# A transformer block in float32: a hand-written engine order for the first norm and for the turn to the up projection

## The chip, the cores and the metric

The kernel runs on one core of a Trainium2 chip. The metric is the device time of one launch in microseconds (us), and of several runs the median. The engines are named as the profile names them: PE is TensorE (PEld its weight loads), DVE is VectorE, ACT is ScalarE, POOL is GpSimd, SP is SyncE, which here only issues DMAs.

## The reference, cut to what matters

One block works on x of 1024 tokens by 1024 channels, all in float32: a norm, one wide projection into a gated convolution, an attention with three dilations and two gates, their merge, a second norm, and a feed-forward part with a short causal convolution.

```python
h = rms_norm(x, norm1_g)                       # first norm
z = h @ w_in
glu_in, q, k, v, gate_logits = split(z)
a = causal_depthwise_conv(a_val * sigmoid(a_gate), conv_w, conv_b)
y_a = silu(rms_norm(a, conv_norm_g)) @ w_conv_out
y_b = dilated_attention(q, k, v) @ w_attn_out
x = x + (g_a * y_a + g_b * y_b) @ w_out
h = rms_norm(x, norm2_g)                       # second norm
u = causal_depthwise_conv(h @ w_up, ffn_conv_w, ffn_conv_b)
x = x + (silu(u_gate) * u_val) @ w_down
```

## The kernel before, in words

**Products.** Each float32 operand is split into a high part (ACT copies it into the type float32r, L76) and a low part (DVE subtracts the high part, L77). A product is three matmuls: high by high, high by low, low by high (gemm_half, L103 to L111; product, L546 to L552). A weight piece of 128 by 1024 is loaded by SP into one of four buffers of the tag "raw" (stage, L79), then split.

**First norm (L197 to L224).** ACT issues a DMA that reads the norm's weights once for each of 128 partitions (gb1, L200). SP loads the eight x tiles of 128 tokens and, after the fourth, the first two weight pieces (g0, v0). For each tile ACT squares with a running sum (L221), DVE forms the mean (L100), POOL takes the power -1/2 (L101), DVE scales by it and by gb1 (L223), PE transposes eight blocks into two PSUM banks (L190), and ACT and DVE split them into the high and low halves of hT.

**Gated convolution input (L227 to L238).** For each of eight channel groups two products, glug and gluv, each in two halves of 512 tokens: half 0 needs the norm's tiles 0 to 3, half 1 tiles 4 to 7. The first channel group uses g0 and v0.

**Output projection and second norm (L522 to L543).** In the second pass over the eight token tiles, each tile's product wo goes through: DVE adds x (L533), ACT squares (L535), DVE and POOL form the factor (L538, L100, L101), DVE scales (L540). Two tiles later PE transposes the scaled tile (L515) and ACT copies it into "raws" (L516). The halves 0 and 1 of raws hold tokens 0 to 511 and 512 to 1023; with the two halves of the channels these are the four blocks b11, b21 (first tokens) and b12, b22 (last tokens).

**Up projection (L546 to L659).** It is computed in the manner of Strassen and Winograd: seven products for a two by two block of products. Its left operands are the sums t1 = b12 - b11, t3 = b22 - b12, t2 = t3 + b11 and t4 = b21 - t2, and b11, b21, b22 themselves (L594 to L621). POOL makes t1 and t4, DVE the others; each is made in two column halves (cols) and split. For each of the 22 channel tiles f, up_first loads the weight uv and makes the two products X and Z; up_sums loads ug and makes with DVE the sums s12 and two differences (s3, and a12, which becomes s4); up_rest makes the other five products, of which two are accumulated onto Y and the others onto X, and the short convolution. The sums s12 sit in a "raw" buffer too.

**Order.** Every engine runs its own queue in order. In what order the instructions are put there is decided by a scheduler when the kernel is built, from the order of the code and from its own estimates.

Of the kernel before, what the change touches and what calls it, by code (L numbers as in the profile page):

```python
# [12 lines left out]
F32 = mybir.dt.float32  # L13
# [37 lines left out]
def block_kernel(ctx: ExitStack, tc: tile.TileContext, x, g1, g2, pack, mask,  # L51
# [38 lines left out]
    def wpiece(src, name):  # L90
        raw = stage(src, name)
        hi, lo = wsplit(raw, name)
# [20 lines left out]
    def gemm_ch(ps, w, actT):  # L113
        for half in range(2):
            for _ in gemm_half(ps[:, half * 512 : half * 512 + 512], w, actT, half):
                pass
# [66 lines left out]
    def transpose_split(dst, src, tt):  # L183

        half, c0 = tt // 4, (tt % 4) * P
        for kk in range(2):
            ps = bank_ps(f"tp_{tt}_{kk}")
            for j in range(4):
                k = kk * 4 + j
                pe.transpose(ps[:, j * P : (j + 1) * P], src[:, k * P : (k + 1) * P], ident)  # L190
            psv = ps.rearrange("p (a b) -> p a b", a=4)
            hi = dst[0][half][:, kk * 4 : kk * 4 + 4, c0 : c0 + P]
            lo = dst[1][half][:, kk * 4 : kk * 4 + 4, c0 : c0 + P]
            split(hi, lo, psv)


    with tc.tile_pool(name="ph1", bufs=1) as p1:  # L197
        t4 = lambda name, dt=F32: p1.tile([P, 1024], dt, tag="t4", bufs=4, name=name)
        gb1 = p1.tile([P, D], F32, tag="csq", bufs=1, name="gb1")
        act.dma_start(gb1, bass.AP(tensor=g1.tensor, offset=g1.offset, ap=[[0, P], [1, D]]))  # L200
        xt = []
        for tt in range(8):
# [3 lines left out]
            if tt == 3:  # L206
                wfirst = [wpiece(w_ch[8], "g0"), wpiece(w_ch[0], "v0")]
        sp.dma_start(pk, pack)
        make_identity(nc, ident)
        pool.memset(mhalf, -0.5)  # L210
        pool.memset(ones, 1.0)
        dve.tensor_tensor(out=qkg, in0=pk[:, C_QG : C_QG + 1], in1=pk[:, C_KG : C_KG + 1], op=ALU.mult)
        dve.tensor_scalar(qkg, qkg, DH ** -0.5, None, op0=ALU.mult)

        hT = hb_tiles(hb1, "hT")
        for tt in range(8):
            xx = xt[tt]
            xs = t4(f"xs_{tt}")
            ss = p1.tile([P, 1], F32, tag="ss", bufs=2, name=f"ss_{tt}")
            rs = p1.tile([P, 1], F32, tag="rs", bufs=2, name=f"rs_{tt}")  # L220
            act.activation(xs, xx, AF.Square, accum_out=ss)  # L221
            rstd_of(rs, ss, D, ss)
            dve.scalar_tensor_tensor(out=xs, in0=xx, scalar=rs, in1=gb1, op0=ALU.mult, op1=ALU.mult)  # L223
            transpose_split(hT, xs, tt)  # L224
# [3 lines left out]
        for c in range(8):  # L228
            a = p1.tile([P, CW - 1 + T], F32, tag="apad", bufs=10, name=f"apad_{c}")
            pool.memset(a[:, : CW - 1], 0.0)  # L230
            gp = big_ps(f"glug_{c}")
            gemm_ch(gp, wfirst[0] if c == 0 else wpiece(w_ch[8 + c], f"g{c}"), hT)
            sg = t4(f"sg_{c}")
            act.activation(sg, gp, AF.Sigmoid)
            vp = big_ps(f"gluv_{c}")
            gemm_ch(vp, wfirst[1] if c == 0 else wpiece(w_ch[c], f"v{c}"), hT)
# [3 lines left out]
        sqacc = p1.tile([P, T], F32, name="sqacc")  # L240
# [233 lines left out]
    with tc.tile_pool(name="ph3", bufs=1) as p3:  # L474
# [46 lines left out]

        tails = []  # L522
        for j in range(2):
            wpieces = [wpiece(w_o[j, :, 2 * i : 2 * i + 2, :], f"wo{j}_{i}") for i in range(4)]
            for tt in range(8):
# [7 lines left out]
                dve.tensor_tensor(out=x2[:, cs], in0=ps, in1=x2[:, cs], op=ALU.add)  # L533
                sp.dma_start(dx2[tt][:, cs], x2[:, cs])
                act.activation(ps, x2[:, cs], AF.Square, accum_out=ss2[:, tt, j : j + 1])  # L535
                if j == 1:
                    s1 = p3.tile([P, 2], F32, tag="s1", bufs=2, name=f"s1_{tt}")
                    dve.tensor_tensor(out=s1[:, 0:1], in0=ss2[:, tt, 0:1], in1=ss2[:, tt, 1:2], op=ALU.add)  # L538
                    rstd_of(s1[:, 1:2], s1[:, 0:1], D, s1[:, 0:1])
                    dve.scalar_tensor_tensor(out=x2, in0=x2, scalar=s1[:, 1:2], in1=gb2, op0=ALU.mult, op1=ALU.mult)  # L540
# [16 lines left out]
        def up_first(f):  # L557

            v = stage(w_up[f], f"uv{f}")
            vh, vl = wsplit(v, f"uv{f}")  # L560
            xz = big_ps(f"xz_{f}")
            product(xz[:, 0:512], four(vh)[:, 0:4], four(vl)[:, 0:4], *left[0], True)
            product(xz[:, 512:1024], four(vh)[:, 4:8], four(vl)[:, 4:8], *left[1], True)
            return v, xz

        def up_sums(f, v):
            g = stage(w_up[FT + f], f"ug{f}")
            s = wp.tile([P, 1024], F32, tag="raw", bufs=4, name=f"s12_{f}")
            a11, a12, a21, a22 = v[:, 0:512], v[:, 512:], g[:, 0:512], g[:, 512:]
            s1, s2 = s[:, 0:512], s[:, 512:]  # L570
            dve.tensor_tensor(out=s1, in0=a21, in1=a22, op=ALU.add)
            dve.tensor_tensor(out=s2, in0=s1, in1=a11, op=ALU.subtract)
            sw = wsplit(s, f"s12_{f}")
            dve.tensor_tensor(out=a21, in0=a11, in1=a21, op=ALU.subtract)
            gw = wsplit(g, f"s3g_{f}")
            dve.tensor_tensor(out=a12, in0=a12, in1=s2, op=ALU.subtract)
# [12 lines left out]
        t2 = []  # L589

        def keep(n, src, q):
# [267 lines left out]
```

## Time and profile before

| | |
|---|---|
| median of 3 runs | 1815.13 us (1812.67 to 1815.44) |
| profiled execution | 1811.43 us, span 1809.6 us |
| granted TensorE clock | 0.991 |
| PE busy | 1765.8 us |
| DVE busy | 1318.8 us |
| ACT busy | 771.6 us |
| POOL busy | 195.8 us |

The span runs from the first to the last instruction. In rows of the timeline the first number is the start in us, the second the length; an "x4" at the end says that four instructions are merged, and the bracket gives the idle time before and what ended it. Rows of stretches give for each engine its busy time and, in brackets, its instructions, then the granted clock, the busy share of the DMA engines and GB/s. Rows of waits give the total, the number and the longest.

### The profile page before, as it was taken

The page shows a single profiled execution, that of the slowest core. Times are in us where ns is not written, and L with a number is a line of the kernel's source. Part 1 is how long each engine was busy: PE and PEld are TensorE (multiplying, and loading weights), DVE is VectorE, ACT ScalarE, POOL GpSimd, SP SyncE. Part 2 cuts the span into 40 slices and gives each one's busy share as a digit, 9 for nine tenths or more (in the row PEclk, how much of TensorE's full clock was granted, in tenths as well). Part 3 has the DMA queues.
Part 4 walks back from the last instruction along what each step waited for, and adds up shares of the span by engine and source line. Part 5 has one row for each costly group of instructions (what it writes and reads, how often), then busy time and mean ns, then how long its engine had stood idle before and what let it go on. Part 6 is the DMA issues. An engine that isn't in the chain of part 4 may idle for free.

```text
span 1809.6 us, 22474 instructions
## 1 busy us (share of the span) xinstructions
PE 1765.8 (98%) x8244; PEld 1461.9 (81%) x8244; DVE 1318.8 (73%) x1798; ACT 771.6 (43%) x1202; POOL 195.8 (11%) x197
## 2 busy tenths in 40 slices
PE   7999999999999999999999999989999999999999
PEld 5888888888887888887888878768888888878887
DVE  5999999999735655666654543787777777789863
ACT  4111132232245656666655332545444554543441
POOL 1000133133002122222210000210000000000000
PEclk9999999999999999999999999999999999999999
DMA  5111145345549456666527543313222222389851
GB/s 203 59 47 47 41 134 163 116 134 157 157 173 246 145 158 175 180 165 179 164 70 279 169 160 133 104 48 107 80 82 81 71 95 91 116 303 335 298 180 47
DMA packets 142063, 257.57 MB, mean 142 GB/s; under 512 B 11265, under 2 KB 60545, under 8 KB 141953
## 3 DMA queue, kind: packets, MB, share of 16 engines
q1 hardware_dynamic: 141808, 255.61, 43.8%
q8 instruction: 65, 1.06, 0.3%
q10 hardware_dynamic: 144, 0.52, 0.1%
q14 instruction: 46, 0.37, 0.1%
HBM read 190.03 MB, written 66.06 MB: 142 GB/s over the span
## 4 chain that ended last, share of the span: by engine, by line
PE 53%; DMA 4%; DVE 4%; issue 1%; ACT 1%; SPq 1%; POOLq 0%; POOL 0%; DVEq 0%; ACTq 0%
PE xz L550 5%; PE xz L551 5%; PE xz L552 5%; PE dx L703 5%; PE dy L703 5%; DMA gg<-dya 2%; PE pp L400 2%; PE y L550 2%; PE y L552 2%; PE y L551 2%; PE ya L108 2%; PE ya L109 2%; PE ya L110 2%; PE o L408 2%; PE wo L126 1%; PE wo L127 1%
## 5 line engine op out<-in xcount | busy, mean ns | idle before, releaser
L253 DVE SCALAR_TENSOR_TENSOR cacc<-apad,pk,cacc 128x1024 f32<-128x1024 f32 x240 | 297.7, 1274 | 0.7
L125 PE MATMUL qkv<-hi_qkv,hT 128*128 128x512 f32 x384 | 151.8, 396 | 0.0
L127 PE MATMUL qkv<-hi_qkv,hT 128*128 128x512 f32 x384 | 150.0, 391 | 0.0
L126 PE MATMUL qkv<-lo_qkv,hT 128*128 128x512 f32 x384 | 149.4, 390 | 0.0
L389 DVE CUSTOM_DVE_ANT_0 p<-s,m 128x128 f32<-128x128 f32 (+7 forms) x128 | 95.1, 750 | 62.7 <-PE pp L400 39.0
L77 DVE TENSOR_TENSOR pl<-pp,ph 128x512 fp32r<-128x512 f32 x192 | 103.1, 549 | 49.1 <-ACT ph L76 48.6
L393 POOL TENSOR_SCALAR p<-p,st 128x128 f32<-128x128 f32 (+7 forms) x128 | 94.9, 748 | 335.5 <-DVE st L392 211.9
L76 ACT ACTIVATE ph<-pp 128x512 fp32r<-128x512 f32 x192 | 91.3, 487 | 92.2 <-PE pp L400 89.3
L649 DVE SCALAR_TENSOR_TENSOR u<-u,pk 128x1023 f32<-128x1023 f32 (+1 forms) x88 | 112.3, 1279 | 18.9 <-ACT u L647 18.5
L101 POOL TENSOR_TENSOR rs<-ss,mhalf 128x8 f32<-128x8 f32 (+1 forms) x40 | 80.3, 2010 | 353.1 <-DVE ss L100 353.0
L391 ACT ACTIVATE p<-p,st 128x128 f32<-128x128 f32 (+7 forms) x128 | 99.0, 776 | 14.6 <-DVE st L389 12.9
L108 PE MATMUL gate<-hT,hi_gt 128*128 128x512 f32 x256 | 101.8, 398 | 0.0
L109 PE MATMUL gate<-hT,hi_gt 128*128 128x512 f32 x256 | 100.8, 394 | 0.0
L110 PE MATMUL gate<-hT,lo_gt 128*128 128x512 f32 x256 | 100.3, 393 | 0.0
L400 PE MATMUL pp<-ident,p 128*128 128x128 f32 x576 | 94.4, 277 | 0.0
L127 PEld LDWEIGHTS qkv<-hi_qkv,hT 128*128 128x128 f32 x384 | 72.0, 188 | 15.3
L126 PEld LDWEIGHTS qkv<-lo_qkv,hT 128*128 128x128 f32 x384 | 72.2, 188 | 14.5 <-DVE lo_qkv L77 0.3
L125 PEld LDWEIGHTS qkv<-hi_qkv,hT 128*128 128x128 f32 x384 | 72.2, 188 | 14.0
L400 PEld LDWEIGHTS pp<-ident,p 128*128 128x128 f32 x576 | 69.5, 142 | 10.0 <-issue 0.2
L384 PE MATMUL s<-kh,q 128*128 128x512 f32 (+1 forms) x192 | 69.7, 368 | 7.3 <-DVE st L389 4.8
L408 PE MATMUL o<-ph,v 128*128 128x512 f32 x192 | 73.1, 381 | 3.6 <-ACT ph L76 1.8
L409 PE MATMUL o<-pl,v 128*128 128x512 f32 x192 | 70.5, 369 | 1.6 <-DVE pl L77 1.5
(269 smaller groups left out, 4610.4 us busy)
## 6 DMA issues: line engine op xcount, KB each, us to landing
wr<-w_down SPq DMA_DIRECT2D x45, 512.0 KB, 5.7
gr<-dff SPq DMA_DIRECT2D x62, 256.0 KB, 5.2
raw_qkv<-w_qkv SPq DMA_DIRECT2D x24, 512.0 KB, 3.9
raw_uv<-w_up SPq DMA_DIRECT2D x22, 512.0 KB, 3.3
raw_ug<-w_up SPq DMA_DIRECT2D x22, 512.0 KB, 3.3
dff<-u SPq DMA_DIRECT2D x22, 512.0 KB, 2.6
dv<-v SPq DMA_DIRECT2D x16, 512.0 KB, 3.2
raw_gt<-w_ch SPq DMA_DIRECT2D x16, 512.0 KB, 4.8
```

The lines of the kernel that those rows point to most:

```text
L108: pe.matmul(o, hi[:, k, :], ah[:, k, :], start=(k == 0), stop=False)
L109: pe.matmul(o, hi[:, k, :], al[:, k, :], start=False, stop=False)
L110: pe.matmul(o, lo[:, k, :], ah[:, k, :], start=False, stop=(k == KT - 1))
L125: pe.matmul(ps, ah, hi[:, k % 2, :], start=(k == 0), stop=False)
L126: pe.matmul(ps, ah, lo[:, k % 2, :], start=False, stop=False)
L127: pe.matmul(ps, al, hi[:, k % 2, :], start=False, stop=(k == KT - 1))
L253: dve.scalar_tensor_tensor(out=acc, in0=a[:, j : j + T], scalar=w(j), in1=acc, op0=ALU.mult, op1=ALU.add)
L400: pe.transpose(pp[:, qb * P : (qb + 1) * P], pts[qb][:, kt * P : (kt + 1) * P], ident)
L550: pe.matmul(o, wh[:, k, :], bh[:, k, :], start=(start and k == 0), stop=False, skip_group_check=not start)
L551: pe.matmul(o, wh[:, k, :], bl[:, k, :], start=False, stop=False, skip_group_check=not start)
L552: pe.matmul(o, wl[:, k, :], bh[:, k, :], start=False, stop=(k == 3), skip_group_check=not start)
L703: pe.matmul(banks[n], a[:, c], b[:, d], start=(start and i == 0 and m == 0), stop=(stop and i == nf - 1 and m == 2), skip_group_check=True)
```

## The change

1. The first norm's weights come as one row on one partition. Two matmuls with a row of ones spread it over the partitions into PSUM, and DVE copies it into gb1 in two pieces.
2. A block with a manual schedule fixes the order on ACT, DVE and PE from there to the last tile's split: statistic, scaling and transposes of tiles 0 to 3, the splits of their first four channel blocks, the products of glug and gluv over these blocks, the other four blocks, and tiles 4 to 7 one by one. The transposes of tile 2 go to PSUM that the first products use later. The weight split of the second channel group is issued after it.
3. At the turn the last tile's addition, the last three transposes, the sums and the first three up products stand in a second manual block. The weights uv0 and uv1 are staged ahead of it. PE's transposes of tile 6 stand before the first up product. The third product (f = 2) goes to two single banks.
4. POOL makes none of the sums any more: DVE makes t1, t2 = b22 - t1, t3 and t4. The low part of b22 is made by ACT (minus the high part) and by two DMAs from the POOL queue that add b22 to it.
5. In up_sums the difference a12 is formed before s3; for f = 0 the work is cut in two.

The diff, cut to its core:

```diff
-        gb1 = p1.tile([P, D], F32, tag="csq", bufs=1, name="gb1")
-        act.dma_start(gb1, bass.AP(tensor=g1.tensor, offset=g1.offset, ap=[[0, P], [1, D]]))
+        g1r = p1.tile([1, D], F32, tag="csq", bufs=1, name="g1r")
+        act.dma_start(g1r, g1.unsqueeze(0))
...
+        with tc.manual_schedule(engines={ENG.Activation, ENG.DVE, ENG.PE}):
+            for kk in range(2):
+                ps = bank_ps(f"gb_{kk}")
+                pe.matmul(ps, ones[0:1, :], g1r[:, kk * 512 : kk * 512 + 512], start=True, stop=True)
+                dve.tensor_copy(gb1[:, kk * 512 : kk * 512 + 512], ps)
+            for tt in range(3):
+                measure(tt)
+                scaled(tt)
+                turned(tt, 0)
+                turned(tt, 1)
+            measure(3)
+            high(0, 0)
+            low(0, 0)
+            scaled(3)
+            high(0, 1)
+            low(0, 1)
+            turned(3, 0)
+            turned(3, 1)
+            for tt in (1, 2):
+                high(tt, 0)
+                low(tt, 0)
...
+            act.activation(hl[0][0], wraw[0], AF.Copy)
+            high(3, 0)
+            low(3, 0)
+            wlow(0)
+            act.activation(hl[1][0], wraw[1], AF.Copy)
+            wlow(1)
+            a, b = range(4), range(4, 8)
+            first_pair(0, a, ((0, 0),), 0)
...
+            for tt in (1, 2, 3):
+                high(tt, 1)
+                low(tt, 1)
+            measure(4)
+            scaled(4)
+            first_pair(0, b, ((0, 0),), 0)
+            first_pair(0, b, ((0, 0), (0, 1)), 1)
+            first_pair(0, b, ((0, 1), (1, 0)), 0)
+            turned(4, 0)
+            turned(4, 1)
+            first_pair(0, b, ((1, 0),), 1)
+            measure(5)
+            scaled(5)
+            for kk in range(2):
+                high(4, kk)
+                low(4, kk)
+            for tt in (5, 6):
+                turned(tt, 0)
+                turned(tt, 1)
+                measure(tt + 1)
+                scaled(tt + 1)
+                for kk in range(2):
+                    high(tt, kk)
+                    low(tt, kk)
+            turned(7, 0)
+            turned(7, 1)
+            for kk in range(2):
+                ends = high(7, kk), low(7, kk)
...
-        v0, xz0 = up_first(0)
-        transpose_raw(*tails.pop(0))
-        ready = [(v0, xz0) + up_sums(0, v0)]
...
+        pre = [stage(w_up[f], f"uv{f}") for f in range(2)]
+        pre = [(v, wsplit(v, f"uv{f}")) for f, v in enumerate(pre)]
+        with tc.manual_schedule(engines={ENG.Activation, ENG.DVE, ENG.PE}):
+            transpose_raw(*tails.pop(0))
+            add_rest(1, 7, x2, ps)
+            transpose_raw(*tails.pop(0))
+            sums(cols[0])
+            s7 = spread(7)
+            high2("t2", t2[0], cols[0])
+            low2("t2", t2[0], cols[0])
+            scale2(x2, s7)
+            v0, xz0 = up_first(0, pre[0])
+            transpose_raw(x2, 7)
+            early2 = up_sums(0, v0, 0)
+            ups = [up_first(1, pre[1]), up_first(2, None, True)]
+            sums(cols[1])
+            high2("t2", t2[1], cols[1])
+            low2("t2", t2[1], cols[1])
+            for q, t in zip(cols, t13):
+                last = high2("t1", t, q), low2("t1", t, q)
+            ready = [(v0, xz0) + up_sums(0, v0, early2)]
...
+            for q in cols:
+                high2("b22", b22[:, :, q], q)
+                lo = blocks["b22"][1][:, :, q]
+                act.activation(lo, blocks["b22"][0][:, :, q].bitcast(F32), AF.Copy, scale=-1.0)
+                pool.dma_start(lo.bitcast(F32), b22[:, :, q], accum_op=ALU.add)
```

In it measure(t) is the square on ACT, the mean on DVE and the power on POOL; scaled(t) is DVE's scaling; turned(t, k) four transposes of a tile; high and low are the two parts of a split; first_pair makes products of the first channel group over the given channel blocks; less, high2 and low2 are a subtraction on DVE and the two parts of a split of the sums.

More of the change, by code (lines that the diff above doesn't have):

```diff
@@ L111, in gemm_half, with gemm_ch @@
             yield
-    def gemm_ch(ps, w, actT):
-        for half in range(2):
+    def gemm_ch(ps, w, actT, halves=(0, 1)):
+        for half in halves:
             for _ in gemm_half(ps[:, half * 512 : half * 512 + 512], w, actT, half):
@@ L599, in sums @@
[L599 to L608 removed]
+            t = t13[q.start // 256]
+            t2.append(view(p4r.tile([P, 1024], F32, tag="st", bufs=2, name=f"cb_t2_{q.start}")))
```

200 lines of the change are left out of this document (121 added, 79 removed).

## The prediction, made before the changed kernel ran

> **What bounds the kernel now.** I read the busy table first, then stretches of the first norm and of the turn to the up projection, then the waits.
>
> ```profile
> span 1809.6 us, 22474 instructions
> PE 1765.8 (98%) x8244; PEld 1461.9 (81%) x8244; DVE 1318.8 (73%) x1798; ACT 771.6 (43%) x1202; POOL 195.8 (11%) x197
> ```
>
> TensorE (PE) is busy for 98% of the span, so the change can gain only where PE waits or runs at half clock. In the stretches the columns are length, then busy time of PE, weight loads, VectorE (DVE), ScalarE (ACT), POOL, then the granted clock.
>
> ```profile
> 9.41:20.18 10.77, 6.95 (x33) 5.58 (x33) 9.51 (x15) 9.61 (x18) 2.12 (x8) 0.85 1.03 419
> 20.18:48.21 28.03, 27.77 (x128) 22.27 (x128) 15.19 (x24) 12.07 (x19) 3.32 (x6) 0.94 0.20 70
> 1202.19:1247.19 45.00, 44.89 (x195) 36.18 (x194) 35.99 (x40) 24.52 (x28) 0.00 (x0) 1.00 0.20 71
> 1158.88:1209.90 51.02, 41.78 (x182) 32.91 (x180) 46.22 (x44) 27.75 (x36) 13.39 (x6) 0.93 0.19 65
> ```
>
> PE's first product begins at 20.18; from there to 48.21, where the second channel's product begins, PE hardly waits. The turn (1158.88 to 1209.90, the first product of up tile 2) holds 46.22 us of DVE work in 51.02: DVE bounds it. After it PE is full again. So time won or lost by 48.21 and by 1209.90 goes straight to the end; both points are the same work in both kernels.
>
> PE's pace, and the links of the norm's chain:
>
> ```profile
> 5.99 1.06 ACT L221 ACTIVATE xs<-x 128x1024 f32<-128x1024 f32 x1 [3.55 <-DMA x<-x]
> 7.17 0.15 DVE L100 TENSOR_SCALAR ss<-ss 128x1 f32<-128x1 f32 x1 [7.17 <-ACT xs L221]
> 8.07 1.28 DVE L223 SCALAR_TENSOR_TENSOR xs<-x,rs,gb 128x1024 f32<-128x1024 f32 x1 [0.75 <-POOL rs L101]
> 17.76 1.94 PE L190 MATMUL tp<-ident,xs 128*128 128x128 f32 x8 [1.94 <-DVE xs L223]
> 20.18 0.80 PE L108 MATMUL glug<-hT,hi_g 128*128 128x512 f32 x1 [0.48 <-ACT hT L76]
> 23.19 0.63 PE L110 MATMUL glug<-hT,lo_g 128*128 128x512 f32 x1
> 23.62 0.49 PE L108 MATMUL glug<-hT,hi_g 128*128 128x512 f32 x1
> 25.10 0.39 PE L108 MATMUL glug<-hT,hi_g 128*128 128x512 f32 x1
> 25.33 0.39 PE L109 MATMUL gluv<-hT,hi_v 128*128 128x512 f32 x1
> 27.60 1.91 PE L190 MATMUL tp<-ident,xs 128*128 128x128 f32 x16
> 28.24 2.06 ACT L76 ACTIVATE hT<-tp 128x512 fp32r<-128x512 f32 x4 [3.42 <-PE tp L190]
> 28.41 1.28 DVE L223 SCALAR_TENSOR_TENSOR xs<-x,rs,gb 128x1024 f32<-128x1024 f32 x1
> 29.61 2.48 DVE L77 TENSOR_TENSOR hT<-tp,hT 128x512 fp32r<-128x512 f32 x4
> 48.21 0.50 PE L108 MATMUL glug<-hT,hi_g 128*128 128x512 f32 x1
> ```
>
> A product costs 0.43 us at half clock (23.19 to 23.62) and 0.227 at full. Eight transposes cost 1.94 and some 0.8 (mean 0.1 each from the 16 in 1.91, the last's tail off). A squared tile reaches DVE 1.18 after its start (5.99 to 7.17); from there to the scaling 0.90, the scaling 1.28. A high part takes ACT 0.52 (four in 2.06), a low part DVE 0.62 (2.48 for four).
>
> **Part 1, the first norm.** *Spread weight.* The 512 KB broadcast goes, one row of 4 KB, two matmuls with ones and two DVE copies come.
>
> ```profile
> gb<-g ACTq DMA_DIRECT2D x1, 512.0 KB, 5.5
> 506.43 0.61 PE L333 MATMUL psr<-dg,ones 128*128 128x128 f32 x4
> 507.94 0.69 DVE L335 COPY sqacc<-psr 128x512 f32<-128x512 f32 x1
> ```
>
> At the stretch's 419 GB/s, 512 KB are 1.25 us: x may land 0 to 1.25 earlier; I take 1.0, so 4.9. The nearest matmuls with ones are two records each; four of 128 columns take 0.61, about 0.45 each at 512 columns, 0.9 a matmul and 1.8 at half clock. The copies (0.69) stand at the head of DVE's queue: with the row landed near 3 the second ends at about 7.3, and DVE's first statistic waits for it instead of 6.1 (4.9+1.18). Bounds 6.1 to 7.4; I take 7.3.
>
> *To the first product.* In the new order each tile is statistic, scaling, next tile: 0.90+1.28, about 2.15 with overlaps. The fourth ends at 7.3 + 3x2.15 + 2.18 = 15.9; four transposes at half clock, 0.25 of pipe and a high part (0.6) bring the first product to 17.6, not 20.18: **2.6 us won** (bounds 1.2 to 4).
>
> *After it.* The new PE order has 44 products, then tile 4's transposes, 4 products, tiles 5, 6, 7, then 48 products. 44x0.227 = 10.0, and 1.4 for the products still at half clock (seven by 0.2), end at 29.0; tile 4's first four transposes at 29.4. Now the queues bite: DVE has tile 6's scaling *behind* tile 4's low parts, and tile 7's behind tile 5's. From 29.4: pipe 0.24, two highs (1.05), the square of tile 6 queued behind them on ACT (1.18), statistic to scaling 0.90, scaling 1.3: tile 6 can be transposed at 34.05. PE has 4 products and 12 transposes till 31.45: it **waits 2.6**. Then two lows (1.25), 0.9 and 1.28: tile 7 at 37.45; PE, done at 34.85, **waits 2.6** again. High and low part of tile 7 let the half-1 products run from 39.15 and, for all but two, 40.05. Before, the last of the eight scalings was done at 29.7 (28.41+1.28), ahead of PE's need, so nothing of this was seen. 46 products take 10.4, with 0.4 for half clock: the second channel begins at 50.9. **Part 1: +2.7** (bounds +0.5 to +4).
>
> The half clock in it:
>
> ```profile
> 13.58:16.99 3.41, 1.07 (x8) 0.86 (x8) 3.41 (x5) 3.41 (x8) 0.66 (x2) 1.00 1.02 415
> 16.99:20.40 3.41, 2.17 (x9) 1.80 (x10) 3.41 (x6) 3.41 (x8) 0.38 (x2) 0.50 1.04 422
> 20.40:23.81 3.41, 3.41 (x8) 2.29 (x9) 3.41 (x7) 3.29 (x7) 0.97 (x3) 0.50 0.59 230
> ```
>
> A window with 1.07 us of PE in 3.41 is followed by half clock until one is full. PE's 0.8 between 31.45 and 34.85 is as little, so tile 7 and the first products run at half clock: 1.0 us of the +2.7. [...]
>
> **Part 2, the turn.** Before, 24 transposes (2.4) and 156 products (35.4) make 37.8 of 51.02 us, so 13.2 are lost.
>
> ```profile
> PE y L551 <- DVE blk_t L77: 4.7, 1, 4.7
> PE y L550 <- ACT hi_s L76: 2.7, 1, 2.7
> 1160.19 2.43 POOL L599 TENSOR_TENSOR cb_t<-h2raw,h2raw 128x1024 f32<-128x1024 f32 x1 [0.55 <-ACT h2raw L516]
> 1160.29 3.41 DVE L540 SCALAR_TENSOR_TENSOR x<-x,s,gb 128x1024 f32<-128x1024 f32 x1
> 1167.18 1.28 DVE L540 SCALAR_TENSOR_TENSOR x<-x,s,gb 128x1024 f32<-128x1024 f32 x1
> 1170.65 2.90 DVE L77 TENSOR_TENSOR lo_s<-raw_uv,hi_s 128x512 fp32r<-128x512 f32 x1
> 1183.83 2.80 DVE L602 TENSOR_TENSOR cb_t<-cb_t,h2raw 128x1024 f32<-128x1024 f32 x1
> 1191.80 2.75 DVE L571 TENSOR_TENSOR s<-raw_ug 128x512 f32<-128x512 f32 x1
> 1165.91 1.04 ACT L76 ACTIVATE hi_uv<-raw_uv 128x1024 fp32r<-128x1024 f32 x1
> 1166.86 1.04 ACT L76 ACTIVATE blk_t<-cb_t 128x1024 fp32r<-128x1024 f32 x1
> 1151.81 3.49 DVE L77 TENSOR_TENSOR h2left<-h2raw,h2left 128x1024 fp32r<-128x1024 f32 x3
> raw_uv<-w_up SPq DMA_DIRECT2D x1, 512.0 KB, 3.4
> ```
>
> *DVE's work.* Beside a POOL subtraction the scaling took 3.41, else 1.28. With POOL's four gone DVE gets them (4x1.14, from 3.49 for three) and loses b22's two low parts (2x1.14, now ACT and an accumulating DMA): 2.3 more. Against it stand the four stretched rows: 3.41 for 1.28, 2.90 and 2.75 where 512 columns take 0.62, 2.80 for 1.14, some 8 us less. That alone shortens the stage by several us. But the new order adds a wait.
>
> *The order, step by step.* Tiles 5 and 6 are transposed together: PE waits 0.55 for tile 6's scaling and its first up product ends at 1166.5; tile 7's scaling is ready at 1166.9, the second product ends at 1173.15. Meanwhile DVE makes the sums of tile 0's weight (1166.8 to 1168.1), ACT splits them behind tile 7's copies (1168.6), DVE makes the low part (1169.7) and a12 (ends 1171.5). **Only now may SP load the third weight, uv2**: in the program it takes the buffer of those sums, which a12 reads last, and SP waits for exactly that instruction. 3.4 us (row above; 0.1 of signal) land it at 1174.95. ACT's next instruction is uv2's high part and DVE's its low part, both queues in order: DVE stands for 4.6 us, ACT from 1169.7, PE for **2.9** (1173.15 to 1176.05) and 0.85 more for the low part. Queued behind on DVE are the second column's subtractions; behind on ACT its high part and eleven more.
>
> *Then.* DVE: low part and two subtractions, 1176.1 to 1179.7. ACT from 1179.75: seven of 1024 columns to 1186.3 (t2, t1 twice, b22 twice, its negative twice, each 0.94), s3g, s4, t4 twice, the copy of X, t3 (0.94, or 0.53 at 512 columns), and at 1191.2 the copy of Y, without which PE may not add b22 to Y. PE's third product (24 of 0.227, the wait and 1.7 of half clock after it) ends at 1184.05, Y's first at 1186.95; PE **waits 4.9**, to 1191.8. The last 72 products take 16.3 and, after the empty window, 3.1 of half clock: the first product of tile 2 comes at 1211.2, against 1209.90. **Part 2: +1.3.** Without the wait for uv2 the same count gives 1206.1, so -3.8: this wait is the step I trust most and the price that matters most. Bounds -3.8 to +4.
>
> *Accumulating DMA.* No row shows one. Issued by 1186.5, it is hidden if it lands by 1191.8, 5.3 us later; the nearest rows are 512 KB in 3.4 and in 5.5, so I take it as hidden; at 10 us it costs 4.1 more. [...]
>
> Elsewhere the instructions are those of before save small swaps in attention's filler: 0, with up to 2 us either way from half-clock windows falling differently.
>
> **Sum.** +2.7 +1.3 = +4.0. The profiled execution took 1811.43 us (span 1809.6), so 1815.4 in its terms; it lies 3.7 below the median of the runs shown, 1815.13, which the forecast is put against: **1819.1 us**.
>
> **Rivals.**
> 1. *The accumulating DMA lands late* (10 us): PE's wait for b22 grows, 1823.2. For it: two halves on a queue no row shows. Against: 5.3 us of room. 13%.
> 2. *The load of uv2 doesn't bind* (landed before ACT is free): part 2 is -3.8, the sum -1.1, 1814.0. It decides at a landing by 1169.7, 5.3 us before mine; each us between costs about one. The order of a12 and the load speaks against, but a dozen links of mine could be off, or DVE be ahead: 19%.
> 3. *Other side: DVE and ACT no longer bound either stage.* Faster if, beside case 2, tiles 6 and 7 are scaled before PE asks, that is if DVE reached them by 31.4; then 5.2 us of waits go and part 1 is -2.5, the sum -6.3, 1808.8. For it: 2.6 us won at the first product. Against: DVE's order. 10%.
> 4. *The clock stays full through part 1's waits*: 1.0 less, 1818.1. The row with 1.07 us speaks against it. [...] 4%.
>
> **How the numbers follow.** The forecast has 54%, reaching from +2 to +6. Cases 1, 2, 4 and it hold 90%; from 1812.5 (case 2 with 1.5 off) to 1825 (case 1 with 2 on) about 8 in 10 lie. A measurement here can tell about 0.2% (3.6 us) from no change. Faster by more: 0.11 (case 3 and a tail of 2). Within: case 2's rest, case 4 and the forecast's lower quarter, 0.36. Slower by more: 0.53.
>
> **What would show it.** Right: PE's first product before 18.5, then two waits of 2 to 3 us ahead of tiles 6 and 7, the second channel after 50; at the turn a DVE gap of 4 to 5 us ending with uv2's low part, with SP's load issued right after a12, and a PE gap before b22 whose releaser is ACT's copy of Y, not the POOL queue; DVE scalings of 1.28 there. Wrong: tiles 6 and 7 without a gap; uv2 landed before DVE is at it; a PE wait released by the accumulating DMA; new gaps in the attention stage.

## The result and the profile after

The changed kernel takes 1826.49 us (median of 6 runs, 1822.79 to 1828.61) against 1815.29 us before (6 runs, 1812.67 to 1817.89): ratio 1.0061, 95% interval 1.0047 to 1.0076, so 8.5 to 13.8 us slower. Forecast were 4.0 us and a range that ended at 1825.0. The sign was right, the size was not.

The profiled execution took 1828.39 us (span 1826.6), that of before 1811.43: 17.0 apart, more than the medians. Both were cut at the same three instructions: the first product of the second channel, the last product of the output projection, the last product of the up projection. The stretches of the changed kernel:

```profile
0.00:51.72 51.72, 39.65 (x164) 29.86 (x164) 28.37 (x41) 26.12 (x41) 5.95 (x24) 0.93 0.45 167
51.72:1168.82 1117.10, 1099.68 (x5288) 913.65 (x5288) 789.24 (x1230) 451.33 (x819) 174.05 (x168) 0.99 0.47 143
1168.82:1611.13 442.31, 429.84 (x1873) 352.44 (x1872) 339.40 (x371) 218.83 (x262) 3.99 (x4) 0.98 0.25 85
```

and those of the kernel before:

```profile
0.00:48.21 48.21, 34.72 (x160) 27.84 (x160) 26.19 (x40) 25.26 (x41) 7.00 (x24) 0.93 0.50 191
48.21:1158.64 1110.43, 1094.42 (x5287) 910.57 (x5288) 790.91 (x1234) 452.05 (x820) 175.21 (x168) 0.99 0.47 144
1158.64:1594.24 435.60, 426.25 (x1873) 350.19 (x1872) 342.17 (x365) 216.30 (x260) 13.63 (x6) 0.99 0.25 85
```

What is left to the end is the down projection, 215.47 and 215.36 us. The start costs 3.5 us more, the stretch of the turn and the up projection 6.7, the last one nothing, and the middle one, where the change moved little, 6.7. In the middle PE has the same 5288 weight loads and is busy 5.3 us longer: the same products, with 27.3 us at half clock where before has 17.1. Where that comes from, the twelve other profiles show below.

**The start.** PE and ACT in the timeline of the changed kernel, from the first product to the second channel:

```profile
17.36 1.16 PE L239 MATMUL glug<-hT,whi_g 128*128 128x512 f32 x4 [0.63 <-DVE hT L233]
23.09 0.60 ACT L230 ACTIVATE hT<-gluv 128x512 fp32r<-128x512 f32 x1 [4.82 <-PE gluv L239]
24.23 1.19 PE L239 MATMUL glug<-hT,whi_g 128*128 128x512 f32 x4 [1.18 <-ACT hT L230]
33.94 1.06 PE L222 MATMUL tp<-ident,xs 128*128 128x128 f32 x8 [2.20 <-DVE xs L214]
37.14 1.94 PE L222 MATMUL tp<-ident,xs 128*128 128x128 f32 x8 [2.14 <-DVE xs L214]
38.91 0.79 PE L107 MATMUL glug<-hT,whi_g 128*128 128x512 f32 x1
42.49 0.44 PE L108 MATMUL glug<-hT,whi_g 128*128 128x512 f32 x1
51.72 0.50 PE L107 MATMUL glug<-hT,hi_g 128*128 128x512 f32 x1
```

The first product comes at 17.36 instead of 20.18. Then PE waits for the scaled tiles 6 (2.20) and 7 (2.14), the transposes of tile 7 take 1.94 for eight, and eight products from 38.91 to 42.49 are 0.45 apart instead of 0.227. One wait was not forecast: ACT stands 4.82 us till 23.09 for products of gluv before it may read a transposed block that lies in the other half of gluv's PSUM tile.

**The turn.** DVE, ACT and PE in the timeline of the changed kernel; the last two rows belong to up tiles 1 and 2:

```profile
1176.11 1.28 DVE L624 SCALAR_TENSOR_TENSOR x<-x,s,gb 128x1024 f32<-128x1024 f32 x1
1181.36 0.68 DVE L681 TENSOR_TENSOR raw_uv<-raw_uv,s 128x512 f32<-128x512 f32 x1
1185.31 1.06 ACT L76 ACTIVATE hi_uv<-raw_uv 128x1024 fp32r<-128x1024 f32 x1 [5.13 <-DMA raw_uv<-w_up]
1186.40 1.23 DVE L77 TENSOR_TENSOR lo_uv<-raw_uv,hi_uv 128x1024 fp32r<-128x1024 f32 x1 [4.36 <-ACT hi_uv L76]
1186.42 0.79 PE L651 MATMUL xzx<-h2left,hi_uv 128*128 128x512 f32 x1 [2.38 <-ACT hi_uv L76]
1201.49 0.58 ACT L772 ACTIVATE p<-y 128x512 f32<-128x512 f32 x1
1202.16 0.47 PE L651 MATMUL y<-blk_b22h,hi_s 128*128 128x512 f32 x1 [4.07 <-issue]
1204.76 0.77 PE L652 MATMUL y<-blk_b22l,hi_s 128*128 128x512 f32 x1 [2.12 <-DMA blk_b22l<-h2raw]
1247.46 0.60 ACT L767 ACTIVATE u<-xzx 128x512 f32<-128x512 f32 x1 [0.38 <-DMA dff<-u]
1248.11 0.50 PE L651 MATMUL xzx<-blk_t,hi_s 128*128 128x512 f32 x1 [1.67 <-ACT u L767]
```

The scaling takes 1.28 now that POOL subtracts nothing (3.41 before). But after a12 (1181.36) the third weight has to be loaded; ACT stands 5.13 us for it and DVE 4.36, PE 2.38. Then PE waits ahead of b22 for ACT's copy of Y (the row says "issue"; the copy ended at 1202.07) and 2.12 more for the accumulating DMA. In tile 2 it waits 1.67 for ACT's copy of X, which waits for the store of tile 0's output, since that output holds the buffer.

To compare the turn in many kernels I counted PE's instructions in the timeline from the last product of the output projection. The 182nd, called point B here (the prediction's point at 1209.90 is the 181st), starts 51.48 us after that product before and 54.78 after; the 600th 147.28 and 153.99.

### The profile page after: what moved, and what is told of

Same layout as the page of the kernel before. It is cut to its first block, busy times and chain, and to the rows that moved or that the text cites. A ratio compares the mean times of both kernels' runs of the same rounds, so it can differ in the third digit from the quotient of the medians.

```text
span 1826.6 us, 22485 instructions
## 1 busy us (share of the span) xinstructions
PE 1779.6 (97%) x8248; PEld 1469.2 (80%) x8248; DVE 1316.6 (72%) x1802; ACT 774.3 (42%) x1204; POOL 184.0 (10%) x195
## 4 chain that ended last, share of the span: by engine, by line
PE 52%; DMA 5%; DVE 3%; ACT 1%; issue 1%; SPq 1%; POOL 0%; DVEq 0%; ACTq 0%
PE xz L653 5%; PE xz L651 5%; PE xz L652 5%; PE dx L839 5%; PE dy L839 5%; PE pp L489 2%; PE y L652 2%; PE y L651 2%; DMA gg<-dya 2%; PE y L653 2%; PE ya L107 2%; PE wo L125 2%; PE ya L108 2%; PE ya L109 2%; PE wo L126 2%; PE wo L124 2%
## 5 line engine op out<-in xcount | busy, mean ns | idle before, releaser
L100 POOL TENSOR_TENSOR rs<-ss,mhalf 128x8 f32<-128x8 f32 x32 | 73.4, 2296 | 339.9 <-DVE ss L99 339.9
```

## The experiments

The table has what the profile of each shows (time of the second channel's first product; length of the middle, up and last stretches) and the ratio of the medians to the kernel before on the same chip, with its 95% interval; a dash stands where there was a single run. In turn_low_by_vector and all_two_first 24 products of the down projection stand ahead of the up projection's last product, so for these two only the sum of the last two stretches can be compared (659.92 and 652.62; turn_only has 656.90, the kernel before 650.96).

| kernel | second channel | middle | up | last | ratio |
|---|---|---|---|---|---|
| before | 48.21 | 1110.43 | 435.60 | 215.36 | 1 |
| the change | 51.72 | 1117.10 | 442.31 | 215.47 | 1.0061 (1.0047 to 1.0076) |
| first_only | 50.93 | 1117.07 | 435.63 | 215.37 | 1.0028 (1.0016 to 1.0040) |
| turn_only | 49.41 | 1108.89 | 441.20 | 215.70 | 1.0023 (1.0013 to 1.0032) |
| first_only_scaled_early | 47.92 | 1114.45 | 435.06 | 215.37 | 0.9995 (0.9984 to 1.0006) |
| first_only_highs_early | 50.17 | 1108.69 | 436.66 | 215.38 | 1.0010 (0.9998 to 1.0021) |
| first_only_both | 44.69 | 1109.38 | 435.56 | 215.37 | 0.9974 (0.9964 to 0.9984) |
| first_both_broadcast | 45.52 | 1114.71 | 435.61 | 215.76 | 0.9992 (0.9979 to 1.0004) |
| turn_sums_early | 49.51 | 1108.09 | 437.43 | 215.67 | - |
| turn_two_first | 48.99 | 1108.82 | 437.02 | 215.47 | - |
| turn_low_by_vector | 49.29 | 1108.49 | 447.36 | 212.56 | - |
| turn_b22_early | 48.67 | 1113.28 | 435.74 | 215.61 | - |
| all_edits | 44.77 | 1112.84 | 436.03 | 215.46 | 0.9989 (0.9978 to 1.0001) |
| all_two_first | 44.86 | 1109.32 | 439.36 | 213.26 | 0.9974 (0.9962 to 0.9987) |

### One part alone

first_only has the new first norm and the old turn, turn_only the reverse; each is the diff of the change cut at the line that makes "raws".

> Only the first norm is as in the changed kernel; the turn is that of before. In the profiles of the two kernels the second channel's product began at 48.21 us and at 51.72 (+3.5); from there to the last product of the output projection PE took 6.7 us more (1110.4 and 1117.1); from that product to the last one of the up projection 6.7 more (435.6 and 442.3); the medians differ by 11.2 only. Theory: the two edits are separate, and the 6.7 in the middle stage is mostly where the half-clock windows happen to fall in one execution. Then this kernel shows 51.7 +-0.3 at the second channel, 435.6 +-0.5 in the last stretch, and its median is 1815.3 + 3.5 = 1818.8 (1817.3 to 1821). Rival: the first norm's new order also slows the middle stage in every execution; then the middle stretch is near 1117 and the median 1822 or more.

> Only the turn is as in the changed kernel; the first norm is that of before. Theory (the edits are separate, the turn alone costs 6.7): second channel at 48.2 +-0.1; 442.3 +-0.7 from the last product of the output projection to the last of the up projection; median 1815.3 + 6.7 = 1822.0 (1820 to 1824). Rival (the turn costs only the 1.3 that was forecast, and the rest is an effect of the first norm's edit): 437 in that stretch, median 1816.6.

Measured: 0.28% and 0.23% slower, 0.51% together, inside the interval of the whole change. first_only's up stretch is that of before to 0.03 us, turn_only's is 5.6 longer (with the last stretch 5.9): the two edits are separate, and the turn costs far more than the 1.3 forecast. first_only itself missed its expectation twice: the second channel came at 50.93 (51.7 +-0.3 expected), and its middle took 1117.07, the rival's number; the other profiles below decide that. The theory's condition on the start of turn_only failed as well: the second channel came at 49.41, not 48.2, with the very instructions of before. Its stretches there, columns as in the prediction:

```profile
16.24:19.65 3.41, 1.94 (x8) 1.57 (x8) 3.41 (x5) 3.41 (x8) 0.12 (x1) 0.50 1.03 418
19.65:23.06 3.41, 3.02 (x7) 2.00 (x8) 3.41 (x9) 3.28 (x7) 1.13 (x3) 0.50 0.78 317
23.06:26.47 3.41, 3.41 (x10) 2.64 (x9) 2.97 (x6) 1.62 (x2) 2.22 (x4) 0.50 0.00 0
```

Before, two stretches ran at half clock (16.99 to 23.81); here the boundaries lie 0.75 us earlier, the second stretch has 3.02 of 3.41 us of work instead of 3.41, and a third one stays at half clock. In six profiles with the old first norm the second channel comes between 48.21 and 49.51, mean 49.0.

The middle stretch shows the same on a larger scale. At the start of the output projection PE waits for the first weights, 2.8 us in the kernel before, 2.6 in the changed one, 0.50 in first_only_both. The changed kernel there, then the kernel before:

```profile
1073.41:1076.82 3.41, 1.44 (x6) 0.62 (x4) 3.19 (x5) 2.19 (x5) 0.00 (x0) 1.00 0.51 193
1076.82:1080.24 3.42, 2.83 (x7) 2.25 (x8) 3.38 (x5) 1.64 (x3) 0.00 (x0) 0.50 0.53 147
1080.24:1083.65 3.41, 3.41 (x10) 2.64 (x9) 0.78 (x2) 0.00 (x0) 0.00 (x0) 0.50 0.85 278
```

```profile
1068.26:1071.68 3.42, 1.72 (x8) 1.27 (x8) 3.37 (x5) 1.58 (x2) 0.00 (x0) 1.00 0.28 57
1071.68:1075.09 3.41, 3.41 (x17) 2.83 (x16) 2.08 (x3) 0.63 (x1) 0.00 (x0) 1.00 0.81 268
```

A stretch with 1.44 us of work is followed by two at half clock, one with 1.72 by none. Over all fourteen profiles the middle takes 1108.1 to 1117.1 us: 1108.1 to 1113.3 (mean 1109.7) with the old first norm, 1108.7 to 1117.1 (mean 1113.0) with the new. The granted clock goes with it: the middle stands at half clock for 17.1 us in the kernel before and for 27.3 in the changed one, and over the whole execution the two profiles at 1117.1 show 0.987 and 0.988, the twelve others 0.991 to 0.994. The 10.2 us more of the changed kernel cost up to half of that, 5.1 us, which nearly covers the 5.3 by which PE is busy longer. So most of the 6.7 in the profiled pair is how long the clock stood at half, and first_only_highs_early and first_only_both show that the new first norm can have the short middle. By the medians first_only_both wins 2.9 to 6.5 us, and its start alone is 4.3 ahead of the mean of the six profiles with the old norm (44.69 and 49.0), so no slower middle shows there. That the new norm shifts the odds by an us or two is not excluded.

### The first norm

first_only_scaled_early:

```diff
-            measure(5)
-            scaled(5)
+            for tt in (5, 6, 7):
+                measure(tt)
+                scaled(tt)
             for kk in range(2):
                 high(4, kk)
                 low(4, kk)
             for tt in (5, 6):
                 turned(tt, 0)
                 turned(tt, 1)
-                measure(tt + 1)
-                scaled(tt + 1)
```

> The first norm as in the changed kernel, turn of before, with one edit: statistics and scalings of tiles 5, 6 and 7 stand ahead of tile 4's high and low parts on ScalarE and VectorE. Theory (tiles 6 and 7 are late only because VectorE has their scaling behind the low parts of the tile before): tile 6 is scaled by about 31.3 and tile 7 by about 33.4 instead of 33.8 and 37.0, PE's waits of 2.2 and 2.1 us ahead of their transposes fall to 0.5 to 1.5 in all, the low parts end near 38, and the second channel's product begins at 46.5 to 48.0 instead of 51.7; median 1813.5 to 1815. Rival (VectorE is short of time there whatever the order): the low parts are late instead, PE's products of the second half wait for them, second channel at 50 or later, median 1817 or more.

Measured: 47.92, inside the span expected, and no difference from before by the medians. Its timeline:

```profile
32.94 4.87 DVE L233 TENSOR_TENSOR hT<-tp,hT 128x512 fp32r<-128x512 f32 x8
33.68 2.45 PE L222 MATMUL tp<-ident,xs 128*128 128x128 f32 x16 [2.39 <-DVE hT L233]
```

The waits for scaled tiles are gone. One of 2.39 takes their place, for tile 4's low part, whose PSUM bank tile 6 needs. The order was the cause of the two waits; what PE waits for next is DVE, which now makes eight low parts without a break (4.87 us).

first_only_highs_early:

```diff
-            wlow(1)
             a, b = range(4), range(4, 8)
             first_pair(0, a, ((0, 0),), 0)
-            first_pair(0, a, ((0, 0),), 1)
             first_pair(0, a, ((0, 1), (1, 0)), 0)
-            first_pair(0, a, ((0, 1), (1, 0)), 1)
             for tt in (1, 2, 3):
                 high(tt, 1)
                 low(tt, 1)
+            wlow(1)
+            first_pair(0, a, ((0, 0),), 1)
+            first_pair(0, a, ((0, 1), (1, 0)), 1)
             measure(4)
```

> The first norm as in the changed kernel, turn of before, with one edit: ScalarE stood 4.8 us and VectorE 3.0 us before 23.1, since tile 2's second high part reads the other half of the PSUM tile that the value branch's first products write, and waits for all of them. Here the gate's 12 first products come first, then that high part and low part are issued ahead of the value branch's 12, with the second weight's low part behind them. Theory: ScalarE goes on at 18.2 instead of 23.1, the square of tile 4 starts near 19.3 instead of 24.06, the wait of 1.2 ahead of the products at 24.2 goes, tiles 6 and 7 are scaled some 4 us earlier (by about 30 and 33), and the second channel begins at 47 to 49; median 1814 to 1816. Rival (the wait was off the path, since VectorE's order of scalings and low parts decides alone): the second channel stays between 50.5 and 51.7, median near 1818.

Measured: 50.17, just under the rival's span and far from the theory's; the rival was right. ACT and PE in its timeline:

```profile
18.75 1.08 ACT L210 ACTIVATE xs<-x 128x1024 f32<-128x1024 f32 x1
27.88 1.09 ACT L230 ACTIVATE hT<-tp 128x512 fp32r<-128x512 f32 x2 [6.93 <-PE tp L222]
32.28 1.06 PE L222 MATMUL tp<-ident,xs 128*128 128x128 f32 x8 [2.20 <-DVE xs L214]
35.49 1.94 PE L222 MATMUL tp<-ident,xs 128*128 128x128 f32 x8 [2.14 <-DVE xs L214]
```

ACT squares tile 4 at 18.75 instead of 24.06, as expected, and then stands 6.93 us for the transposes of tile 4; tile 6's square is queued behind their high parts. Tiles 6 and 7 come as late after tile 5 as ever, 2.20 and 2.14.

first_only_both has both edits.

> The first norm as in the changed kernel with both edits at once (tiles 5 to 7 measured and scaled ahead of tile 4's high and low parts; tile 2's second high and low part issued ahead of the value branch's products), turn of before. One alone gave a second channel at 47.92 us, the other alone 50.17, both against 50.93 to 51.72 with neither. Theory: with the squares begun at 18.75 and nothing between them, the four scalings end near 23.5, 25.6, 27.7 and 29.7, the eight low parts run from 29.7 to 34.6, PE waits 1 to 2 us for the PSUM buffers of tiles 6 and 7 and the second channel begins at 44.5 to 46.0; median 2.5 to 3.5 us under before. Rival (the highs issued early bring nothing once the scalings stand first): 47.5 to 48.5, the same as before.

Measured: 44.69, ratio 0.9974. The two edits gain 6.2 us on first_only together, 3.0 and 0.8 alone: the one left the early idle time of ACT, the other the order of the queue. (The 0.8 is no more than the difference between the changed kernel and first_only, 51.72 and 50.93, with the same first norm.) PE waits 0.22 ahead of tiles 6 and 7:

```profile
16.92 2.08 PE L239 MATMUL glug<-hT,whi_g 128*128 128x512 f32 x8 [0.63 <-DVE hT L233]
30.23 2.45 PE L222 MATMUL tp<-ident,xs 128*128 128x128 f32 x16 [0.22 <-DVE hT L233]
44.69 0.50 PE L107 MATMUL glug<-hT,hi_g 128*128 128x512 f32 x1
```

first_both_broadcast takes back the spread by matmuls alone (the two matmuls and the two copies go too):

```diff
-        g1r = p1.tile([1, D], F32, tag="csq", bufs=1, name="g1r")
-        act.dma_start(g1r, g1.unsqueeze(0))
+        gb1 = p1.tile([P, D], F32, tag="csq", bufs=1, name="gb1")
+        act.dma_start(gb1, bass.AP(tensor=g1.tensor, offset=g1.offset, ap=[[0, P], [1, D]]))
...
```

> The kernel with both edits of the first norm (second channel at 44.69 us, ratio 0.9974 to before), but with the norm weight spread as before, by a 512 KB broadcast, in place of the 4 KB row, the two matmuls with ones and the two copies. Theory: x's first tile lands at 5.9 as before instead of 4.0, but VectorE's copies had held its first statistic till near 6.7 anyway, so the first scaling moves by 0.5 only (8.07), the weights and x's later tiles come 1.2 us later, and the second channel begins 0.5 to 1.3 us later, at 45.2 to 46.0. Rival A (the spread is what won the 2.6 us at the first product): 47 or more. Rival B (worth nothing, the chain of scalings has slack): 44.7 +-0.2.

Measured: first product and second channel

```profile
17.77 2.08 PE L238 MATMUL glug<-hT,whi_g 128*128 128x512 f32 x8 [0.63 <-DVE hT L232]
45.52 0.50 PE L107 MATMUL glug<-hT,hi_g 128*128 128x512 f32 x1
```

0.85 and 0.83 later. Of the 3.3 us between 20.18 and 16.92 the spread gives 0.85; the rest is the order. (The ratio moved by more, 0.9992 against 0.9974; the profile shows the middle at 1114.71 against 1109.38.)

### The turn

turn_sums_early: tile 0's weight sums, the scaling of token tile 7 and a12 stand ahead of the first column's sums. The diff shows the order; up_sums0, which makes the sums and a12, is up_sums for tile 0 in other pieces.

```diff
             transpose_raw(*tails.pop(0))
+            sums0 = up_sums0(pre[0][0])
+            scale2(x2, spread(7))
+            early2 = up_sums0(pre[0][0], sums0)
             sums(cols[0])
-            s7 = spread(7)
             high2("t2", t2[0], cols[0])
             low2("t2", t2[0], cols[0])
-            scale2(x2, s7)
             v0, xz0 = up_first(0, pre[0])
             transpose_raw(x2, 7)
-            early2 = up_sums(0, v0, 0)
```

> The turn as in the changed kernel, first norm of before, with one edit: tile 0's weight sums and their subtraction a12, for which the load of the third weight uv2 waits, stand ahead of the first column's sums on VectorE. Theory (the wait for uv2 delays ScalarE and VectorE by 4.4 to 5.1 us, and with them all that follows): the load goes out some 5 us sooner, PE's wait ahead of the third product (2.3) goes, the copy of Y and the accumulating DMA come 4 to 5 us sooner, and the stretch from the last product of the output projection to the last of the up projection falls from 441.2 (442.3 in the changed kernel) to 436 to 438. Rival (the wait only shifts idle time, and b22's copies and DMA end at the same time): 440.5 or more.

Measured: 437.43, 3.8 less than turn_only. ACT's high part of the third weight no longer waits for its load, nor PE for that. PE's waits that stay:

```profile
PE y L565 <- DMA blk_b22l<-h2raw: 4.5, 1, 4.5
PE y L564 <- issue: 2.3, 1, 2.3
PE xzx L564 <- ACT u L692: 1.4, 1, 1.4
```

turn_two_first:

```diff
-            ups = [up_first(1, pre[1]), up_first(2, None, True)]
+            ups = [up_first(1, pre[1])]
```

> The turn as in the changed kernel, first norm of before, with one edit: only two first products (tiles 0 and 1) stand ahead of the rest of tile 0, as before, so that the third weight's load holds up nothing and tile 2's products come in their old place. Theory: ScalarE and VectorE lose their gap of 4.4 to 5.1 us, but PE loses 5.4 us of cover, so PE waits 5 to 7 us ahead of Y's first product instead of 2.3 ahead of the third; the late waits in tile 2's part (2.8 us in all, most of it for the store of tile 0's output that still holds a buffer) go; the stretch is 438.5 to 441. Rival (the third product is worth its 5.4 us): 443 or more.

Measured: 437.02, 4.2 less than turn_only and under the span expected. Not taking the third product early is about as good as loading for it in time. PE's waits:

```profile
PE y L564 <- ACT blk_t L616: 3.5, 1, 3.5
PE y L564 <- issue: 2.8, 1, 2.8
PE y L565 <- DMA blk_b22l<-h2raw: 1.3, 1, 1.3
```

At point B it is 0.3 us behind turn_only (53.95 and 53.68), at the 600th instruction 4.2 ahead (148.70 and 152.88): none of the late waits in tiles 1 and 2 is left.

turn_low_by_vector:

```diff
-                act.activation(lo, blocks["b22"][0][:, :, q].bitcast(F32), AF.Copy, scale=-1.0)
-                pool.dma_start(lo.bitcast(F32), b22[:, :, q], accum_op=ALU.add)
+                dve.tensor_tensor(out=lo, in0=b22[:, :, q], in1=blocks["b22"][0][:, :, q].bitcast(F32), op=ALU.subtract)
```

> The turn as in the changed kernel, first norm of before, with one edit: b22's low parts are subtracted by VectorE (two instructions of 1024 columns) in place of ScalarE's two negative copies and the accumulating DMAs. Theory (the DMA landed 2.1 us after PE asked in one profile and 4.4 in the other, and the two negative copies delay the copy of Y by 1.9): PE's waits ahead of b22 fall from 6.2 and 6.7 us to 1.5 to 3.5, and the stretch falls from 441.2 to 436 to 438.5. Rival (VectorE's 2.3 us more make the next weights or t4 late, and the gain is given back): 440 or more, with PE waiting for a low part of VectorE.

Measured: point B at 54.14, 0.5 later than turn_only, and PE waits for the same operand from DVE, as the rival said. At the end of the up projection two waits come that no other turn but the last one below shows (the first row is from the waits at the turn, the others from those at the end):

```profile
PE y L565 <- DVE blk_b22l L663: 3.3, 1, 3.3
PE dx L751 <- ACT gh_b L76: 2.2, 1, 2.2
PE dx L751 <- ACT u L691: 1.4, 1, 1.4
```

But by the 600th instruction this kernel is 0.9 ahead of turn_only (151.93 and 152.87), and it loses that and 3.0 more at the end of the up projection, where the scheduler made another order for the last tiles; that was not tried further. So the accumulating DMA is late, but taking it away gains only 0.9 us by the 600th instruction, with two subtractions of 1.14 us (the prediction's count) put on DVE. Which way is better in the end is not shown.

turn_b22_early: turn_sums_early, with b22's buffers exchanged for t3's and these lines, which go from their old place behind t3:

```diff
             ups = [up_first(1, pre[1]), up_first(2, None, True)]
+            for q in cols:
+                high2("b22", b22[:, :, q], q)
+                lo = blocks["b22"][1][:, :, q]
+                act.activation(lo, blocks["b22"][0][:, :, q].bitcast(F32), AF.Copy, scale=-1.0)
+                pool.dma_start(lo.bitcast(F32), b22[:, :, q], accum_op=ALU.add)
```

> The turn with tile 0's weight sums early (stretch 437.43), first norm of before, with one more edit: b22's high parts, negative copies and accumulating DMAs are issued right after uv2's high part, where ScalarE stood idle for 3.7 us; b22's buffers change places with t3's for it. Theory (what is left of the loss is PE's waits ahead of b22, 2.3 for the copy of Y and 4.5 for the DMA, which come late only because ScalarE reaches b22 at 1177.4): the DMAs are issued near 1174 and land before 1183, the copy of Y comes 3.8 us sooner, PE waits 0.5 to 1.5 ahead of b22 in all and loses no half-clock stretch after it; the stretch falls to 429.5 to 432.5, under the 435.6 of before. Rival (VectorE is the bound there whatever ScalarE does, since it was busy from 1171 to 1195 but for 2 us): PE waits for t3's or t4's low parts or the next weights instead, 435 or more.

all_edits is the same with both edits of the first norm.

> The changed kernel with all four reorderings: both of the first norm, tile 0's weight sums early and b22 early. Theory (the stages add): second channel at 44.7, the stretch from the last product of the output projection to the last of the up projection as in the kernel with b22 early alone (429.5 to 432.5), so 3.5 + 3 to 6 = 6.5 to 9.5 us under before: ratio 0.9948 to 0.9964. Rival (the turn's edits bring nothing with the late waits in tile 2's part): as with the first norm's edits alone, 0.9964 to 0.9984.

Measured: 435.74 and 436.03, as before the change and not under it; ratio of all_edits 0.9989, by which nothing can be told from 1. PE's waits in all_edits:

```profile
PE y L652 <- DVE lo_s L77: 2.5, 1, 2.5
PE xzx L650 <- ACT u L779: 1.7, 1, 1.7
```

The wait for the DMA is gone, and point B comes at 48.42, 3.1 us ahead of before. DVE's low part (2.5) is in that already. Behind point B, by the 300th instruction, 2.9 of the 3.1 are lost (79.17 and 79.28), 2.8 of them to four waits of 0.2, 0.4, 1.7 and 0.5, the longest for the copy that waits for tile 0's store; the changed kernel has the same four. So the rival had the number, but only half the cause: DVE limits what point B gains, and the late waits of the third early product take it back.

all_two_first: both edits of the first norm, turn_two_first, and the same five lines of b22 behind "ups", with the same exchange of buffers.

> Both edits of the first norm, and a turn with only two first products ahead (stretch 437.0 alone) and b22's high parts, negative copies and DMAs issued where ScalarE stood idle for 4.3 us, ahead of the second column's high parts. What it tells apart: with the three first products, the same move of b22 gained 3 us at the first product of tile 2 but all of it went in late waits (1.4 to 1.7 for ScalarE's copy behind the store of tile 0's output, 0.5, 0.4, 0.2 and 1.1). Theory (these late waits come with the third early product, as tile 2 then asks for its buffer too soon): here they are gone, PE's waits of 2.8 and 1.3 ahead of b22 shrink to 0.5 to 2.5 (VectorE's low part of s4 last), the stretch is 432.5 to 434.5, 1 to 3 us under before, and with the 3.5 of the first norm the ratio to before is 0.9965 to 0.9975. Rival (VectorE's work, not the buffer, sets when tile 2 can run, so what is won at b22 is lost later in any order): 435.5 or more, and the ratio that of the first norm's edits alone, 0.9974 to 0.9985.

Measured: ratio 0.9974, as with the first norm's edits alone, so the number is the rival's. At the 600th instruction it is 1.7 ahead of before (145.60 and 147.28), and still at the 1800th (417.60 and 419.28), so the theory on the late waits held. But two waits at the change to the down projection take it back (the last two stretches together are 1.7 longer than before):

```profile
PE dx L839 <- ACT gh_b L76: 2.8, 1, 2.8
PE dx L839 <- ACT u L779: 1.4, 1, 1.4
```

No version has a lower ratio than first_only_both, which leaves the turn as it was: 1807.03 against 1811.82 us, 0.9974 (0.9964 to 0.9984). It beats both kernels, since the changed one stands at 1.0061 to the same reference.

## Why the prediction was right and wrong

- **What bounds it.** Right: PE-bound, with DVE in order at both places. Wrong was "After it PE is full again. So time won or lost by 48.21 and by 1209.90 goes straight to the end". Point B was 3.3 us late (1.3 forecast), the 600th instruction 6.7. Of the 3.4 between, 2.8 are waits in tiles 1 and 2 (0.2, 0.4, 1.7 and 0.5 in the changed kernel, and the product after the 1.7 took 0.50 where those ahead of it took 0.39) that belong to the third early product; turn_two_first has none of them. This is the largest term missed, and it was missed because the stage was followed only as far as one reference point.
- **The load of uv2**, the step trusted most: right. ACT stood 5.13 us, DVE 4.36 (4.6 forecast), PE 2.38 (2.9). Undone in two ways it gives back 3.8 and 4.2 us of the up stretch.
- **The copy of Y**: right. PE waited 4.07 for it (4.9).
- **"Accumulating DMA. ... so I take it as hidden"**: failed. It was issued when forecast (27.4 us after the output projection's last product, 27.9 forecast), but its second half landed 7.5 us after its own issue, where the forecast had 5.3 of room, and PE waited 2.12 us for it, 4.4 and 4.5 in turn_only and turn_sums_early. That is rival 1, which had 13% and 10 us. What would have hidden it is ACT's idle time: issued there, no PE wait is put down to it (turn_b22_early, all_edits).
- **Part 1**: +2.7 forecast, 3.5 in the profiled pair, and 2.3 between the means of two and six profiles (51.3 and 49.0). First product 17.6 forecast, 17.36 measured; the waits ahead of tiles 6 and 7 2.6 and 2.6, measured 2.20 and 2.14; the cause, the order of scalings and low parts, shown by first_only_scaled_early and first_only_both. Missed were ACT's 4.82 us for a PSUM tile, and the half clock was undersized: 1.0 forecast, 2.7 by the rows (0.9 on eight transposes, 1.8 on eight products). That tile 4's transposes began at 28.90 (29.0 forecast) is partly luck: the 1.4 of half clock forecast for the first products did not come (the products from 18.36 to 21.98 came 0.226 apart), and a wait of 1.18 for ACT's high part, behind the 4.82, took its place. Rival 4, a clock that stays full through the waits, was wrong: it was half from 35.74 to 42.56.
- **The spread weight**: DVE's second copy was done at 7.14 (7.3 forecast), the first product 2.8 earlier for order and spread together (2.6 forecast). The spread's own share, not forecast apart, is 0.85.
- **"Elsewhere ... 0, with up to 2 us either way"**: too narrow. The profiled pair shows 6.7, and the same stretch varies by 9 us between profiles, and the time at half clock in it is 17.1 us before and 27.3 after.
- **The sum.** Start 2.3 to 3.5 and turn 5.9 to 6.8 make 8.2 to 10.3, against 8.5 to 13.8 by the medians. Whether the rest, at most a few us, is chance or a middle stretch that the new start makes slower on average stays open.

## What to carry to other kernels

Follow a hand-made order past the place it was made for: what it asks for early (a third product) holds a buffer, and the wait (1.67 us here) turns up two tiles later. A wait for a load whose buffer another engine reads last stops all that is queued behind it (ACT stood 5.13 us, DVE 4.36, PE 2.38), so either the reader goes first or the consumer goes later; both gave 4 us here. Two waits that hide each other show only half their price alone, so the pair has to be tried too (0.8 and 3.0 alone, 6.2 together).

## What the runs showed of the hardware

**The accumulating DMA** moved 197 GB/s. In the changed kernel, the DMAs of b22's low part by their tile, and a stretch in which nothing else was loaded:

```profile
DMA to landing us min/median/max: 5.3/6.4/7.5
```

```profile
1200.00:1203.00 3.00, 0.47 (x1) 0.19 (x1) 3.00 (x4) 3.00 (x5) 0.00 (x0) 1.00 1.24 197
```

Plain loads ran at 415 to 422 GB/s in the prediction's stretches. At 197 the two halves of 512 KB take 5.3 us one after the other, an estimate from that rate; they landed 5.3 and 7.5 us after their issue. What slows them, no run here shows.

**The half clock** fell differently on the same instructions: at the start it lasted from 16.99 to 23.81 in the kernel before and from 16.24 to 26.47 in turn_only, and the second channel came 1.2 us apart (48.21 and 49.41). The 3.41 us ahead of a half clock were not idle: 1.07 us of work stood in them in the kernel before (13.58 to 16.99), 1.44 in the changed one (1073.41 to 1076.82). These busy times give no limit: after 1.67 in 3.41 the clock stayed full in all_edits (1228.17 to 1231.58), after 1.73 it was half in turn_b22_early (659.40 to 662.80), after the 1.72 above it stayed full. At half clock, a stretch with 3.02 was followed by another in turn_only (19.65 to 23.06), one with 3.31 by the full clock in the kernel before (552.89 to 556.30).
